# A two-network forward pass on one core: head norms through exp and ln, level sums on VectorE, a skip term on ScalarE, and projections into both kinds of PSUM banks

## The chip, the cores and the metric

The kernel runs on one core of a Trainium2 chip. The metric is device time in microseconds, the median of three runs. A core has five engines that matter here: TensorE (PE in the profile; its weight loads are PEld), VectorE (DVE), ScalarE (ACT), GpSimd (POOL) and SyncE (SP), which only issues DMAs. Each works through its own queue in order, and they meet through semaphores.

## The reference, cut to what matters

The input is 256 tokens of width 1024. Two networks run one after the other, in float32. The first has two layers, each of FFN, mixer, FFN; the mixer of its first layer is a chunked gated linear attention with 4 heads (called the first attention here), that of its second a stick-breaking attention. The second network has one block, in which an S5 state-space branch and an mLSTM branch (4 heads) run from one input projection and are gated and mixed, and then an expert FFN that gathers 16 experts per head for each token. The parts that the change touches:

```
log_a = log_sigmoid(gk_lr @ w_gk2 + b_gk) / 16             # first attention, decay
o = rmsnorm(o, o_norm)                                     # per head, 256 wide
o = o * silu(g);  return o @ w_out
...
h = norm(h) * norm_g + skip * xc                           # mLSTM, per head
y = y * sigmoid(y @ w_glu + b_glu)                         # S5 branch
mixed = sigmoid(g_s) * (y_s @ w_ssm_out) + sigmoid(g_m) * (y_m @ w_ml_out)
```

## The kernel before, in words

Activations lie with the features on the 128 partitions and the 256 tokens along the free axis. All weights come by DMA in pieces of up to 1 MB into two `raw` buffers (`weights`, L145) and are split there into a high and a low part: ScalarE copies the high part `whi` (L198), VectorE subtracts it to get `wlo` (L199). Each of the two has four buffers of 1024 columns. A projection (`acc`, L171) is three matmuls per 128 rows: high by high (L177), high weight by low activation (L178), low weight by high activation (L179). So a piece of weights passes ScalarE, then VectorE, then TensorE.

PSUM is cut into two rings: `bank` (tag `p`, 5 tiles) and `accum` (tag `acc`, 2 tiles). Projections write one or the other; the next user of a tile waits for its evacuation.

The program is written in a natural order, and a scheduler puts each engine's instructions into a fixed queue; `issue_after` holds an instruction behind a named one. What an engine does while it waits is therefore decided before the run.

The first attention (`gla`, L344). The gate's log-sigmoid (`log_sigmoid`, L322) gives P, the sums of the log decays; S starts at zero. Then come 8 levels (l = 0 to 7), each for blocks of B = 2^l tokens: ScalarE takes `eq` and `ek` as exp of half of P and half of S (L417, L418), VectorE and GpSimd scale q and k with them into `qt` (L419) and `kt` (L420), TensorE multiplies them (`put`, L393) and VectorE copies the masked part into s0 and s1 (L394). For the next level, GpSimd adds P's last column of a block to S (L426), and after it VectorE adds it to P (L428). The projections of q, k and v, and of the four gates g, are placed between. After the levels, `weigh` multiplies the scores with v for each of the 4 heads (L441, L442), `rstd256` (L455) squares and sums over the head (L459 to L462), takes the square root on ScalarE (L465) and the reciprocal on VectorE (L469), and `head_norm` (L472) multiplies and splits the result into yh and yl for the output projection. The gates g pass through Silu (L451).

The second block (`block2`, L1112). The S5 scan is 67 steps of five small GpSimd additions and products (L862 to L866), in one chain of its own; its states are copied by ScalarE (`vc`, L875) and multiplied by TensorE into `sy` (L883, L885). Beside it, the mLSTM (`mlstm`, L950) goes through its 4 heads; `third` multiplies the normed head and adds the skip term `sx` (L1096, L1097), then splits it (L1099, L1100). `sx` is computed on VectorE for heads 0 to 2 and on GpSimd for head 3, where also `myl` (L1100) of heads 2 and 3 is made. After the heads come the projections mix and gm (`in_proj`, L908), the S5 output's gate `gl` (one tile for two halves, L1135 reads each half), and ml_out, ssm_out and w_out. After this block the expert part gathers rows `uv` from memory with GpSimd-issued DMAs (L1342).

Of the kernel before, what the change touches and what calls it, by code (L numbers as in the profile page):

```python
# [17 lines left out]
T = 256  # L18
# [14 lines left out]
class Net:  # L33
# [49 lines left out]
    def accum(self, shape, name):  # L83

        return self.ps.tile(shape, F32, tag="acc", name=name, bufs=2)

# [257 lines left out]
    def gla(self, st, x, gnext):  # L344
# [16 lines left out]
        self.log_sigmoid(P, z, self.V("gla_b_gk", 0, 4), [128, 4, T])  # L361
# [47 lines left out]
        for l in range(8):  # L409
# [11 lines left out]
            if l < 7:  # L421
# [4 lines left out]
                nc.gpsimd.tensor_tensor(Sv[:, :, 0, :], Sv[:, :, 0, :],  # L426
# [10 lines left out]
        def weigh(h):  # L437
            ps = self.bank([128, 2, T], name="ov")
            for c in range(2):
                cc = slice(h * 256 + c * 128, h * 256 + (c + 1) * 128)  # L440
                nc.tensor.matmul(ps[:, c, :], v[0][:, cc], s0[:, h, :], start=True, stop=False)  # L441
                nc.tensor.matmul(ps[:, c, 128:256], v[1][:, cc], s1[:, h, :], start=False, stop=True)  # L442
            return ps, self.rstd256(ps)

        weighed = []
        for h in range(4):
            if h % 4 == 0:
                weighed += [weigh(i) for i in range(h, h + 4)]
            for _ in ahead[h]:
                pass  # L450
            nc.scalar.activation(gated[h], gated[h], AF.Silu)  # L451
            self.head_norm(*weighed[h], h, y, gated[h])
        return self.out_proj("gla_w_out", y, x, gnext)

    def rstd256(self, o, e=None):  # L455
# [8 lines left out]
        if e is None:  # L464
            nc.scalar.activation(r, ms, AF.Sqrt, bias=self.eps)  # L465
        else:
            nc.vector.scalar_tensor_tensor(r, ms, 1e-36, e, op0=OP.max, op1=OP.add)
            nc.scalar.activation(r, r, AF.Sqrt)
# [439 lines left out]
    def in_proj(self, st, b0, nb, full, out, fn=None):  # L908
# [4 lines left out]
        for b in range(nb):  # L913
# [6 lines left out]
            else:  # L920
                ps = self.accum([128, 2, T], "ip")
# [28 lines left out]
    def mlstm(self, st, u4):  # L950
# [139 lines left out]
        def third(h, hh, dn):  # L1090
            r = self.rstd256(hh, dn)
            nc.vector.tensor_tensor(hh, hh, r.unsqueeze(1).to_broadcast([128, 2, T]), OP.mult)
            for d in range(2):
                n = 2 * h + d
                sx = self.t2([128, T], "sx")
                (nc.gpsimd if h == 3 else nc.vector).tensor_scalar(sx, xc(n)[:, NM:], self.V("ml_skip", n), None, op0=OP.mult)  # L1096
# [15 lines left out]
    def block2(self, st, x, gnext):  # L1112
# [16 lines left out]
        for b in range(2):  # L1129
            wt = self.weights("ssm_glu", b)  # L1130
            ps = self.bank([128, 2, T], name="gl")
            sg = self.t2([128, 2, T], "sg")
            for j in range(2):
                self.acc(ps[:, j, :], wt, j, lambda k: (yh[:, k, :], yl[:, k, :]))
                nc.scalar.activation(sg[:, j, :], ps[:, j, :], AF.Sigmoid, bias=self.V("ssm_b_glu", 2 * b + j))  # L1135
            nc.vector.tensor_tensor(by4(sg), by4(sg), y[:, 2 * b:2 * b + 2], OP.mult)
            self.split(y2h[:, 2 * b:2 * b + 2, :], y2l[:, 2 * b:2 * b + 2, :], sg)
        for b in range(4):
            wt = self.weights("ml_out", b)
            ps = self.accum([128, 2, T], "mo")  # L1140
# [4 lines left out]
        for b in range(4):  # L1145
            wt = self.weights("ssm_out", b)
            ps = self.accum([128, 2, T], "so")
# [396 lines left out]
```

## Time and profile before

| what | value |
|---|---|
| median of three runs | 1969.02 us (1961.47 to 1969.13) |
| the profiled execution, its own time | 1956.61 us |
| its span | 1954.8 us |
| busy: TensorE, VectorE, ScalarE, GpSimd | 1771.9, 1352.9, 848.2, 657.6 us |
| DMA | 493.53 MB, 252 GB/s in the mean |

The page gives the busy time of each engine and the span in 40 slices. The timelines give each instruction's start and length; the brackets at the end of a line say how long the engine stood idle before it, and what released it. Times in the views count from the start of the span. The first attention lies at about 198 to 312 us, the second block at about 1000 to 1270, the experts from there to the end.

### The profile page before, as it was taken

The page shows a single profiled execution, that of the slowest core. Times are in us where ns is not written, and L with a number is a line of the kernel's source. Part 1 is how long each engine was busy: PE and PEld are TensorE (multiplying, and loading weights), DVE is VectorE, ACT ScalarE, POOL GpSimd, SP SyncE. Part 2 cuts the span into 40 slices and gives each one's busy share as a digit, 9 for nine tenths or more (in the row PEclk, how much of TensorE's full clock was granted, in tenths as well). Part 3 has the DMA queues.
Part 4 walks back from the last instruction along what each step waited for, and adds up shares of the span by engine and source line. Part 5 has one row for each costly group of instructions (what it writes and reads, how often), then busy time and mean ns, then how long its engine had stood idle before and what let it go on. Part 6 is the DMA issues. An engine that isn't in the chain of part 4 may idle for free.

```text
span 1954.8 us, 31080 instructions
## 1 busy us (share of the span) xinstructions
PE 1771.9 (91%) x11905; PEld 1433.5 (73%) x11905; DVE 1352.9 (69%) x2499; ACT 848.2 (43%) x1385; POOL 657.6 (34%) x835
## 2 busy tenths in 40 slices
PE   8999999999999999999999989988777878778776
PEld 7999889999999998899998879963323424334322
DVE  6765678975666567776678465787767676777755
ACT  5444635554544456554444555453222222232223
POOL 4001323041350100200144870245554455555552
PEclk9999999999999999999999999999999999999999
DMA  5555534555654563265465225599999999999996
GB/s 205 191 187 187 182 108 154 198 192 178 213 178 154 191 202 130 89 236 179 167 216 163 71 97 172 184 371 419 420 420 419 419 420 420 420 419 420 420 420 267
DMA packets 81444, 493.53 MB, mean 252 GB/s; under 512 B 14432, under 2 KB 16736, under 8 KB 29072
## 3 DMA queue, kind: packets, MB, share of 16 engines
q0 software_dynamic: 37152, 268.45, 33.2%
q1 hardware_dynamic: 36608, 219.78, 32.7%
q10 hardware_dynamic: 7536, 3.31, 0.8%
q8 instruction: 94, 1.54, 0.3%
q14 instruction: 54, 0.44, 0.1%
HBM read 489.05 MB, written 2.13 MB: 251 GB/s over the span
## 4 chain that ended last, share of the span: by engine, by line
PE 50%; DMA 29%; DVE 8%; POOL 7%; ACT 3%; issue 3%; SPq 0%; ACTq 0%; POOLq 0%; DVEq 0%
DMA uv<-in_peer_uv,route 25%; PE o L177 4%; PE up L177 4%; PE up L179 4%; PE up L178 4%; PE o L179 4%; PE o L178 4%; PE gate L177 4%; PE gate L179 4%; PE gate L178 4%; DVE wlo L199 2%; PE acc L1390 2%; DVE uv L1370 2%; ACT whi L198 1%; POOL V L866 1%
## 5 line engine op out<-in xcount | busy, mean ns | idle before, releaser
L199 DVE TENSOR_TENSOR wlo<-raw,whi 128x1024 fp32r<-128x1024 f32 (+3 forms) x445 | 511.5, 1164 | 188.1 <-ACT whi L198 184.5
L1390 PE MATMUL acc<-uv,dg 128*128 128x512 f32 x1016 | 481.5, 622 | 135.1 <-ACT dg L1388 135.0
L198 ACT ACTIVATE whi<-raw 128x1024 fp32r<-128x1024 f32 (+3 forms) x445 | 424.0, 974 | 359.6 <-PE gate L178 71.9
L1390 PEld LDWEIGHTS acc<-uv,dg 128*128 128x128 f32 x1016 | 190.8, 196 | 420.0 <-ACT dg L1388 222.2
L1342 POOL DMA_INDIRECT uv<-in_peer_uv,route x254 | 325.4, 1281 | 324.7 <-DMA uv<-in_peer_uv,route 196.1
L1370 DVE SCALAR_TENSOR_TENSOR uv<-uv,xn 128x1024 f32<-128x1024 f32 x256 | 313.3, 1224 | 152.7 <-DMA uv<-in_peer_uv,route 149.2
L177 PE MATMUL gate<-xp,whi 128*128 128x256 f32 x704 | 198.4, 282 | 6.8 <-ACT whi L198 6.4
L179 PE MATMUL gate<-xp,wlo 128*128 128x256 f32 x704 | 197.6, 281 | 3.7 <-DVE wlo L199 3.7
L1378 ACT ACTIVATE route<-route 128x2 f32<-128x2 f32 x129 | 26.2, 203 | 400.6 <-DVE uv L1370 400.6
L178 PE MATMUL gate<-xp,whi 128*128 128x256 f32 x704 | 197.2, 280 | 0.5 <-DVE xp L204 0.4
L179 PE MATMUL o<-hh,wlo 128*128 128x256 f32 x704 | 194.8, 277 | 0.0
L179 PE MATMUL up<-xp,wlo 128*128 128x256 f32 x704 | 194.8, 277 | 0.0
L178 PE MATMUL o<-hl,whi 128*128 128x256 f32 x704 | 194.7, 277 | 0.0
L177 PE MATMUL o<-hh,whi 128*128 128x256 f32 x704 | 194.7, 277 | 0.0
L177 PE MATMUL up<-xp,whi 128*128 128x256 f32 x704 | 194.6, 276 | 0.0
L178 PE MATMUL up<-xp,whi 128*128 128x256 f32 x704 | 194.6, 276 | 0.0
L229 POOL TENSOR_TENSOR sumsq<-x 128x256 f32<-128x256 f32 x9 | 6.1, 680 | 412.3 <-DVE x L318 233.8
L177 PEld LDWEIGHTS gate<-xp,whi 128*128 128x128 f32 x704 | 134.5, 191 | 7.9 <-ACT whi L198 6.7
L179 PEld LDWEIGHTS gate<-xp,wlo 128*128 128x128 f32 x704 | 134.3, 191 | 5.0 <-DVE wlo L199 5.0
L178 PEld LDWEIGHTS gate<-xp,whi 128*128 128x128 f32 x704 | 134.5, 191 | 1.2 <-DVE xp L204 1.1
L177 PEld LDWEIGHTS up<-xp,whi 128*128 128x128 f32 x704 | 132.4, 188 | 0.0
L177 PEld LDWEIGHTS o<-hh,whi 128*128 128x128 f32 x704 | 132.3, 188 | 0.0
(459 smaller groups left out, 3782.3 us busy)
## 6 DMA issues: line engine op xcount, KB each, us to landing
raw<-in_ffn_w_up SPq DMA_DIRECT2D x44, 1024.0 KB, 4.8
raw<-in_ffn_w_down SPq DMA_DIRECT2D x64, 704.0 KB, 4.1
raw<-in_ffn_w_gate SPq DMA_DIRECT2D x43, 1024.0 KB, 4.8
raw<-in_w_in SPq DMA_DIRECT2D x18, 1024.0 KB, 4.8
raw<-in_gla_in SPq DMA_DIRECT2D x8, 1024.0 KB, 4.9
raw<-in_sb_in SPq DMA_DIRECT2D x8, 1024.0 KB, 4.8
raw<-in_peer_q SPq DMA_DIRECT2D x8, 1024.0 KB, 8.2
raw<-in_gla_v SPq DMA_DIRECT2D x4, 1024.0 KB, 4.8
```

Of the source, the lines that this page charges most:

```text
L177: nc.tensor.matmul(ps, hi, xh, start=start and n == 0, stop=False)
L178: nc.tensor.matmul(ps, hi, xl, start=False, stop=False)
L179: nc.tensor.matmul(ps, lo, xh, start=False, stop=stop and n == len(steps) - 1)
L198: return (self.nc.scalar.activation(h, src, AF.Copy).ins, self.nc.vector.tensor_tensor(l, src, h.bitcast(F32), OP.subtract).ins)
L199: self.nc.vector.tensor_tensor(l, src, h.bitcast(F32), OP.subtract).ins)
L229: g.tensor_tensor(q, src, src, OP.mult)
L866: g.tensor_tensor(y, y, t[:, 1], OP.add)
L1342: nc.gpsimd.indirect_dma_start(out=out, out_offset=None, in_=table, in_offset=bass.IndirectOffsetOnAxis(ap=ids, axis=0))
L1370: lastdot = nc.vector.scalar_tensor_tensor(u, u, 1.0, xn[i], op0=OP.mult, op1=OP.mult, accum_out=dots[:, k:k + 1]).ins
L1378: gelu = nc.scalar.activation(w[:, ks], dots[:, ks], AF.Gelu_apprx_tanh).ins
L1390: lastv = nc.tensor.matmul(acc[i][b], dg, vt[:, b * 512:(b + 1) * 512], start=False, stop=hd == 7 and k == 14).ins
```

## The change

Six edits, three in the first attention and three in the second block:

- `log_sigmoid` in `gla` is held behind an explicit load of the ScalarE table set number 6, which follows the square root of the norm before.
- The level sums S (L426) move from GpSimd to VectorE.
- The head norms of the first attention take the reciprocal root as exp(-0.5 ln(ms + eps)), both on ScalarE, under the same table set, loaded behind the Silu of gate 1. The Silu of gates 2 and 3 is held behind the last of these exps. `rstd256` stays for the mLSTM alone.
- Head 3's `sx` in the mLSTM moves from GpSimd to ScalarE.
- The projections of `in_proj` (those without the extra tokens), ml_out and ssm_out take `accum` and `bank` in turn (`either`).
- The two halves of `gl` are two tiles.

```diff
+    def either(self, b, shape, name):
+        return self.bank(shape, name=name) if b % 2 else self.accum(shape, name)
...
-        self.log_sigmoid(P, z, self.V("gla_b_gk", 0, 4), [128, 4, T])
+        with self.tc.issue_after(self.load_tables(6, st.sqrt).ins):
+            self.log_sigmoid(P, z, self.V("gla_b_gk", 0, 4), [128, 4, T])
...
-                nc.gpsimd.tensor_tensor(Sv[:, :, 0, :], Sv[:, :, 0, :],
+                nc.vector.tensor_tensor(Sv[:, :, 0, :], Sv[:, :, 0, :],
                                         Pv[:, :, 1, B - 1:B].to_broadcast([128, n, B]), OP.add)
...
-            return ps, self.rstd256(ps)
-
+            return ps
+
+        for h in range(2):
+            for _ in ahead[h]:
+                pass
+            silu = nc.scalar.activation(gated[h], gated[h], AF.Silu).ins
+        tables = self.load_tables(6, silu).ins
         weighed = []
         for h in range(4):
-            if h % 4 == 0:
-                weighed += [weigh(i) for i in range(h, h + 4)]
-            for _ in ahead[h]:
-                pass
-            nc.scalar.activation(gated[h], gated[h], AF.Silu)
+            ps = weigh(h)
+
+            sq = self.t2([128, 2, T], "hsq")
+            nc.scalar.activation(sq, ps, AF.Square)
+            ms = self.bank([128, T], name="hms")
+            nc.vector.tensor_tensor(sq[:, 0, :], sq[:, 0, :], sq[:, 1, :], OP.add)
+            nc.tensor.matmul(ms, self.ones256, sq[:, 0, :], start=True, stop=True)
+            r = self.t2([128, T], "hr")
+            with self.tc.issue_after(tables):
+                nc.scalar.activation(r, ms, AF.Ln, bias=self.eps)
+                lastr = nc.scalar.activation(r, r, AF.Exp, scale=-0.5).ins
+            weighed.append((ps, r))
+        for h in range(4):
+            if h >= 2:
+                for _ in ahead[h]:
+                    pass
+                with self.tc.issue_after(lastr):
+                    nc.scalar.activation(gated[h], gated[h], AF.Silu)
             self.head_norm(*weighed[h], h, y, gated[h])
...
-                ps = self.accum([128, 2, T], "ip")
+                ps = self.either(b, [128, 2, T], "ip")
...
-                (nc.gpsimd if h == 3 else nc.vector).tensor_scalar(sx, xc(n)[:, NM:], self.V("ml_skip", n), None, op0=OP.mult)
+                if h == 3:
+                    nc.scalar.activation(sx, xc(n)[:, NM:], AF.Copy, scale=self.V("ml_skip", n))
+                else:
+                    nc.vector.tensor_scalar(sx, xc(n)[:, NM:], self.V("ml_skip", n), None, op0=OP.mult)
...
-            ps = self.bank([128, 2, T], name="gl")
+            ps = [self.bank([128, T], name="gl") for _ in range(2)]
...
-                self.acc(ps[:, j, :], wt, j, lambda k: (yh[:, k, :], yl[:, k, :]))
-                nc.scalar.activation(sg[:, j, :], ps[:, j, :], AF.Sigmoid, bias=self.V("ssm_b_glu", 2 * b + j))
+                self.acc(ps[j], wt, j, lambda k: (yh[:, k, :], yl[:, k, :]))
+                nc.scalar.activation(sg[:, j, :], ps[j], AF.Sigmoid, bias=self.V("ssm_b_glu", 2 * b + j))
...
-            ps = self.accum([128, 2, T], "mo")
+            ps = self.either(b, [128, 2, T], "mo")
...
-            ps = self.accum([128, 2, T], "so")
+            ps = self.either(b, [128, 2, T], "so")
```

The scheduler sets the queues anew. At three places they differ as follows; the line numbers of the change are higher than those of before (wlo is L203 there, whi L202).

VectorE in the level loop of the first attention, levels 1 to 3, before and then changed:

```order
L419 TENSOR_TENSOR qt_2322<-q,eq 128x256x2
L199 TENSOR_TENSOR wlo<-raw,whi 128x1024
L428 TENSOR_TENSOR P<-P 128x256x2
L199 TENSOR_TENSOR wlo<-raw,whi 128x1024
L428 TENSOR_TENSOR P<-P 128x128x4
L375 TENSOR_TENSOR k<-qk,rstd 128x512
L199 TENSOR_TENSOR wlo<-raw,whi 128x1024
L428 TENSOR_TENSOR P<-P 128x64x8
L199 TENSOR_TENSOR wlo<-raw,whi 128x1024
```

```order
L380 TENSOR_TENSOR k<-qk,rstd 128x512
L203 TENSOR_TENSOR wlo<-raw,whi 128x1024
L431 TENSOR_TENSOR S<-S,P 128x256x2
L433 TENSOR_TENSOR P<-P 128x256x2
L203 TENSOR_TENSOR wlo<-raw,whi 128x1024
L431 TENSOR_TENSOR S<-S,P 128x128x4
L433 TENSOR_TENSOR P<-P 128x128x4
L380 TENSOR_TENSOR k<-qk,rstd 128x512
L203 TENSOR_TENSOR wlo<-raw,whi 128x1024
L431 TENSOR_TENSOR S<-S,P 128x64x8
L433 TENSOR_TENSOR P<-P 128x64x8
L203 TENSOR_TENSOR wlo<-raw,whi 128x1024
```

S now stands on VectorE, right ahead of each P; the splits wlo keep their places between the levels.

ScalarE at the head norms of the first attention (s is s0, hsq the squares, hr the norm, hms its mean square, yh the high part for the output projection), before and then changed:

```order
L451 ACTIVATE g<-g 128x512
L434 ACTIVATE s_2784<-sc 128x4x128
L459 ACTIVATE hsq<-ov 128x512
L465 ACT_TABLE_LOAD
L465 ACTIVATE hr<-hms,eps 128x256
L459 ACTIVATE hsq<-ov 128x512
L198 ACTIVATE whi<-raw 128x1024
L465 ACTIVATE hr<-hms,eps 128x256
L459 ACTIVATE hsq<-ov 128x512
L198 ACTIVATE whi<-raw 128x1024
L465 ACTIVATE hr<-hms,eps 128x256
L459 ACTIVATE hsq<-ov 128x512
```

```order
L453 ACTIVATE g<-g 128x512
L505 ACT_TABLE_LOAD
L439 ACTIVATE s_2785<-sc 128x4x128
L460 ACTIVATE hsq<-ov 128x512
L466 ACTIVATE hr<-hms,eps 128x256
L467 ACTIVATE hr<-hr 128x256
L460 ACTIVATE hsq<-ov 128x512
L202 ACTIVATE whi<-raw 128x1024
L466 ACTIVATE hr<-hms,eps 128x256
L467 ACTIVATE hr<-hr 128x256
L460 ACTIVATE hsq<-ov 128x512
L466 ACTIVATE hr<-hms,eps 128x256
```

The table load has moved ahead of the copy of s0, and each hr has become two rows.

ScalarE around the last mLSTM head and the S5 states (V are the scan's states, its first and second half), before and then changed:

```order
L1099 ACTIVATE myh<-hh 128x512
L468 ACTIVATE hr<-hr 128x256
L198 ACTIVATE whi<-raw 128x1024
L927 ACT_TABLE_LOAD
L927 ACTIVATE mix<-mix 128x512 x2
L1099 ACTIVATE myh<-hh 128x512
L198 ACTIVATE whi<-raw 128x1024 x2
L927 ACTIVATE mix<-mix 128x512
L875 ACTIVATE vc<-V_12149 128x16x31
L875 ACTIVATE vc<-V_12150 128x16x33
```

```order
L202 ACTIVATE whi<-raw 128x1024
L1117 ACTIVATE sx<-xc,vecs 128x256
L1122 ACTIVATE myh<-hh 128x512
L488 ACTIVATE hr<-hr 128x256
L1117 ACTIVATE sx<-xc,vecs 128x256
L202 ACTIVATE whi<-raw 128x1024
L947 ACT_TABLE_LOAD
L947 ACTIVATE mix<-mix 128x512
L202 ACTIVATE whi<-raw 128x1024 x2
L947 ACTIVATE mix<-mix 128x512
L1122 ACTIVATE myh<-hh 128x512
L202 ACTIVATE whi<-raw 128x1024
L895 ACTIVATE vc<-V_12151 128x16x31
```

The two sx are new ahead of the sigmoids of mix. On GpSimd, the two rows of sx that stood between the scan's last addition and myl are gone:

```order
L865 TENSOR_TENSOR V_12150<-V_12150,s5t 128x32
L866 TENSOR_TENSOR V_12150<-V_12150,s5t 128x32
L1096 TENSOR_SCALAR sx<-xc,vecs 128x256 x2
L1100 TENSOR_TENSOR myl<-hh,myh 128x512 x2
L229 TENSOR_TENSOR sumsq<-x_84 128x256
```

```order
L885 TENSOR_TENSOR V_12152<-V_12152,s5t 128x32
L886 TENSOR_TENSOR V_12152<-V_12152,s5t 128x32
L1123 TENSOR_TENSOR myl<-hh,myh 128x512 x2
L233 TENSOR_TENSOR sumsq<-x_84 128x256
L236 TENSOR_TENSOR sq<-x_84 128x256
```

What stays there is myl, behind the scan as before.

## Rows read from the trace of the kernel before

**Rows 1.** page, busy time of the span, then granted TensorE clock and DMA share by slice
```profile
PE 1771.9 (91%) x11905; PEld 1433.5 (73%) x11905; DVE 1352.9 (69%) x2499; ACT 848.2 (43%) x1385; POOL 657.6 (34%) x835
...
PEclk9999999999999999999999999999999999999999
DMA  5555534555654563265465225599999999999996
```

**Rows 2.** chain that ended last in order of time: start us, us, engine, work
```profile
1340.00 18.27 DMA uv<-in_peer_uv,route
```

**Rows 3.** timeline of PE: start, us, engine, line, op, out<-in, count [idle before <-releaser]
```profile
236.85 0.50 PE L192 MATMUL v<-wlo,xp 128*128 128x512 f32 x1 [1.29 <-DVE wlo L199]
...
256.12 2.97 PE L393 MATMUL sc<-qt,kt 128*128 128x128 f32 x16 [2.15 <-DVE v L195]
...
1151.60 0.36 PE L177 MATMUL ip<-xp,whi 128*128 128x256 f32 x1 [1.61 <-DVE mix L925]
...
1166.25 0.58 PE L179 MATMUL ip<-xp,wlo 128*128 128x256 f32 x1 [5.66 <-DVE wlo L199]
...
1173.64 0.27 PE L885 MATMUL sy<-vc,ca 64*64 64x64 f32 x1 [1.59 <-ACT vc L875]
...
1207.13 0.39 PE L177 MATMUL gl<-yh,whi 128*128 128x256 f32 x1 [2.12 <-ACT sg L1135]
...
1242.22 0.36 PE L177 MATMUL so<-yh,whi 128*128 128x256 f32 x1 [1.66 <-DVE mt L1151]
```

**Rows 4.** busy time by stretch: from:to, us, each engine's busy us (instructions), PEclk, DMA share, GB/s
```profile
223.45:234.40 10.95, 10.95 (x50) 8.83 (x48) 6.46 (x7) 5.12 (x7) 5.99 (x5) 1.00 0.47 154
234.40:250.23 15.83, 12.90 (x53) 9.41 (x53) 11.05 (x13) 9.35 (x13) 5.15 (x6) 1.00 0.37 126
258.00:260.00 2.00, 2.00 (x12) 2.00 (x11) 2.00 (x4) 0.00 (x0) 0.83 (x1) 0.50 0.63 160
300.00:312.00 12.00, 9.59 (x71) 8.61 (x72) 9.93 (x18) 5.78 (x9) 0.00 (x0) 1.00 0.20 68
1166.20:1171.20 5.00, 4.95 (x22) 4.77 (x22) 3.44 (x3) 3.57 (x5) 1.13 (x1) 0.50 0.64 215
```

**Rows 5.** timeline of VectorE (DVE)
```profile
234.97 0.69 DVE L428 TENSOR_TENSOR P<-P 128x512 f32<-128x512 f32 x1 [3.60 <-POOL S L426]
...
286.63 1.75 DVE L469 RECIPROCAL hr<-hr 128x256 f32<-128x256 f32 x1 [2.64 <-ACT hr L465]
...
1130.31 1.24 DVE L199 TENSOR_TENSOR wlo<-raw,whi 128x1024 fp32r<-128x1024 f32 x1 [0.31 <-ACT whi L198]
...
1162.68 0.70 DVE L1097 SCALAR_TENSOR_TENSOR hh<-hh,vecs,sx 128x256 f32<-128x256 f32 x1 [10.03 <-POOL sx L1096]
```

**Rows 6.** timeline of GpSimd (POOL)
```profile
230.32 3.52 POOL L420 TENSOR_TENSOR kt<-k,ek 128x512 f32<-128x512 f32 x2 [1.41 <-DVE k L375]
...
240.03 1.08 POOL L426 TENSOR_TENSOR S<-S,P 128x512 f32<-128x512 f32 x1 [1.99 <-ACT ek L418]
...
1130.54 1.12 POOL L866 TENSOR_TENSOR V<-V,s5t 128x32 f32<-128x32 f32 x1
...
1160.24 0.26 POOL L866 TENSOR_TENSOR V<-V,s5t 128x32 f32<-128x32 f32 x1
...
1161.71 1.84 POOL L1096 TENSOR_SCALAR sx<-xc,vecs 128x256 f32<-128x256 f32 x2
```

**Rows 7.** timeline of ScalarE (ACT)
```profile
212.95 1.28 ACT L330 ACT_TABLE_LOAD   x1
...
241.87 0.63 ACT L417 ACTIVATE eq<-P 128x512 f32<-128x512 f32 x1 [0.96 <-DVE P L428]
...
286.12 0.47 ACT L465 ACTIVATE hr<-hms,eps 128x256 f32<-128x256 f32 x1
...
1169.59 4.00 ACT L875 ACTIVATE vc<-V 128x496 f32<-128x496 f32 x4
...
1256.29 0.51 ACT L203 ACTIVATE xp<-x,vecs 128x256 fp32r<-128x256 f32 x1 [0.56 <-DVE x L318]
```

More of the change, by code (lines that the diff above doesn't have):

```diff
@@ L442, in weigh, with rstd256 @@
                 nc.tensor.matmul(ps[:, c, 128:256], v[1][:, cc], s1[:, h, :], start=False, stop=True)
-            return ps, self.rstd256(ps)
+            return ps
[4 more added lines that the diff above has]
+        tables = self.load_tables(6, silu).ins
         weighed = []
         for h in range(4):
-            if h % 4 == 0:
-                weighed += [weigh(i) for i in range(h, h + 4)]
-            for _ in ahead[h]:
-                pass
-            nc.scalar.activation(gated[h], gated[h], AF.Silu)
+            ps = weigh(h)
[15 more added lines that the diff above has]
+                    nc.scalar.activation(gated[h], gated[h], AF.Silu)
             self.head_norm(*weighed[h], h, y, gated[h])
         return self.out_proj("gla_w_out", y, x, gnext)
-    def rstd256(self, o, e=None):
+    def rstd256(self, o, e):
         nc = self.nc
@@ L463, in rstd256 @@
         r = self.t2([128, T], "hr")
[L464 to L468, printed above, removed]
+        nc.vector.scalar_tensor_tensor(r, ms, 1e-36, e, op0=OP.max, op1=OP.add)
+        nc.scalar.activation(r, r, AF.Sqrt)
         nc.vector.reciprocal(r, r)
```

## The prediction

> **What bounds the kernel now.** I read the page first: TensorE is busy for 91% of the span and its clock is full almost throughout, while the DMA engines are full only from the 27th slice on [rows 1]. The chain of waits, read next, shows the same split: up to the gathers it runs mostly through TensorE and what TensorE waits for, and then through the gathers of expert rows, in steps such as 18.27 us [rows 2]. The change touches only the first part. The gathers start when the routes exist, so what TensorE's path loses or saves before them moves the whole second part. The price of each edit is therefore the TensorE time that it frees, and I list TensorE's own waits [rows 3] and the stretches in which it falls behind its rate [rows 4]. At full clock the 48 matmuls of 512 columns of one half of v take 10.95 us [rows 4], 0.228 each; one of 256 columns I count as half of that, 0.114.
>
> The profiled execution took 1956.6 us (span 1954.8). The median of the three runs shown is 1969.0, 12.4 above it, with runs from 1961.5 to 1969.1. I work out a difference on the profiled one and take it from the median.
>
> **The level sums (L426).** In each level GpSimd adds to S once ScalarE's ek has read it, and VectorE's addition to P waits for GpSimd. The weights of v are split on VectorE between these additions, so v's matmuls run at the loop's pace: the first half of v took 10.95 us, the second 15.83 [rows 4], with TensorE waiting for wlo [rows 3]. GpSimd idles 1.99 before an S and takes 1.08 for it, a period of 3.07; once S stood behind two kt products of 3.52 together, and VectorE waited 3.60 for it [rows 5, 6]. The change removes seven GpSimd additions and adds seven on VectorE. Their nearest row is P's addition, same shape and stride, 0.69 [rows 5]; GpSimd's 1.08 is the upper bound, and below 0.69 I see no reason. A level is then eq 0.63 [rows 7], ek as much, overlapping to about 1.2, then S and P 1.4: 2.6 us. A split feeds 12 matmuls, 12 x 0.228 = 2.74. So the loop becomes slightly faster than TensorE, and the second half of v should take 10.95 plus 0.6 for the small transposes of rstd instead of 15.83: **4.3 us** less, ends 2 (a level stays at 3.07 and only the long wait goes) and 4.3.
>
> After v, TensorE waited 2.15 us for v's evacuation, which stood behind a split whose weights had not landed, and then ran at half clock (granted 0.50) [rows 3, 4]: 16 score products took 2.97 us, which at 0.114 are 1.8, and the next projections lose about 0.4, together 1.5. With the splits earlier, the evacuation follows v at once; that is up to 3.7. But from there VectorE has the masked copies, the scalings and the splits of the score stage to do, and no longer a stalled TensorE to catch up with. I take 2 off: **1.7**, ends 0 and 3.7.
>
> **Log-sigmoid.** Two of three table loads of 1.28 us go from ScalarE [rows 7], and exp and ln run back to back. No TensorE wait names them, so alone this is worth nothing; its cover is the projections of q and k. It lets the level loop begin some 2.6 us earlier, which helps the 4.3.
>
> **The head norms.** Four reciprocals of 1.75 us leave VectorE [rows 5]; four exps come to ScalarE, each about the square root's 0.47 [rows 7], and ln takes the square root's place at the same price; ends for each 0.4 and 0.7 (the double shape's 0.63). The table load moves ahead of the copy of s0, while TensorE still multiplies scores and gates. What is late next: the exp of the last head stands behind a split that waits for a weight buffer, then come a Silu table load, the third and fourth gates, and the last yh. From 300 to 312 us TensorE issued 71 matmuls in 12.00 us [rows 4]; they are 8.1 of work, so 3.9 are lost. The last two gates' own chain (scaling, Silu, product, norm, split) still ends behind TensorE, since the second Silu load is still there. I take half: **2.0**, ends 0 and 3.9.
>
> **The last head's skip term.** GpSimd's two sx, 1.84 us together, stand behind the S5 scan; VectorE waited 10.03 us for them [rows 5, 6], TensorE 5.66 for the split behind that, then ran at half clock, and its S5 output (sy) began in earnest only at 1173.64 [rows 3]. On ScalarE an sx costs about the 0.51 of a scaled copy of the same shape [rows 7] (GpSimd's 0.92 at most). Then TensorE's projections finish: the 22 to 23 that were left at 1160.5 take 2.6 us at full clock, less the 1.61 that TensorE waited for a bank before them [rows 3]: 1161.5. What is late next is the scan. Its last step that is read ends at 1160.5. Beside a split of 1.24 us a scan operation took 1.12 instead of 0.26 [rows 5, 6]; three splits now run beside its end: 3 x 0.87 = 2.6, so 1163.1. Of the four copies vc (4.00 [rows 7]) the first can go early; three and a sigmoid of 0.6 remain: sy starts at 1166.7, 6.9 earlier. TensorE idles 5 us before it; after a like pause the clock was at half, and those 23 matmuls took 5.0 us [rows 4] instead of 2.6, so I charge sy 2.4. **4.5**, ends 0 and 9.
>
> The Trainium skill, SBUF — State Buffer, section "Who interferes with whom", speaks against this part: a VectorE instruction with two SBUF inputs locks out a GpSimd instruction that reads SBUF until it has finished. By it every split and every two-input step of the last head would hold the scan for its full length, an estimated 5 us instead of 2.6, and the sum below would be 12.7 instead of 15.1. The trace agrees that the scan is held, but shows 0.87 of a split of 1.24.
>
> **Both kinds of banks.** The wait of gl for sg (2.12 [rows 3]) is one for ScalarE's read of the other half of the same tile; separate tiles take it away: 2.1. The wait of 1.66 before the last blocks of ssm_out [rows 3] is for an accumulator that VectorE's mt empties; the mt itself is no earlier than VectorE's queue lets it be, and the next projection needs its product, so I count 0.5 of it. **2.6**, ends 0 and 3.8. The bank ring of five gets more users; its cover is that the head norms and the gate products have released theirs by then. The order of the DMA queue is the same.
>
> Sum: 4.3 + 1.7 + 2.0 + 4.5 + 2.6 = **15.1 us, say 15**: 1969.0 - 15 = **1954.0**.
>
> **Rivals.** (1) VectorE becomes the bound. It takes 7 x 0.69 = 4.8 us more in the first attention and at the scan's end holds GpSimd. Then v gives 2, the score stage and the norms nothing, the scan 1.7 and the banks 2.1: 5.8, so 1963.2. For it: VectorE's waits for ScalarE and TensorE stay. Against it: 7 us of reciprocals and the long waits leave its queue. (2) A new ring of waits in the level loop, slower than before. If the split ahead of ek on ScalarE waits for a weight buffer that TensorE frees only after the wlo queued behind S on VectorE, a level takes 12 matmuls 2.74, whi 1.0, eq and ek 1.2, S and P 1.4, wlo 1.2: 7.5 instead of 3.07. Over the five levels beside v that is +22, while the other parts give 10.8: 1980. It decides from a level of 5.2 us on. Against it: there are four buffers of either half, and ScalarE's eq waited only for P [rows 7]. (3) The change doesn't do what it says: the freed time is waited away at the next weight or at the gathers, 1969. Against it: the DMA engines are half idle in that part [rows 1].
>
> **Chances.** Forecast 0.60, rival 1 0.25, rival 2 0.05, rival 3 0.10. About 0.5% (10 us) is what a measurement of this kernel can tell from no change. Nearly all of the forecast's own range, 1946 to 1960, is faster than that, and rival 1 is now and then. Hence faster 0.62, same 0.32, slower 0.06. The upper ends add up to 4.3 + 3.7 + 3.9 + 9 + 3.8 = 24.7, the lower to 2; within that, and with the spread of the runs, I give 1943 to 1966, which leaves out rival 2, most of rival 3 and a rest.
>
> **What would show it.** A level period near 2.6 us and no TensorE wait for wlo in v; no half clock at 258; no 10-us wait of VectorE, and sy 4 to 7 us earlier, counted from the projections before it; wider scan steps at its end; no wait of gl for sg. I am wrong if TensorE has new waits for VectorE in the score stage, if sy starts less than 3 us earlier, or if the first gathers do not start 10 us earlier.

## The result, and the profile after

| | before | changed |
|---|---|---|
| median of 20 runs (us) | 1967.07 | 1951.27 |
| lowest to highest (us) | 1959.71 to 1978.77 | 1946.59 to 1965.62 |
| profiled execution's own time, span (us) | 1956.61, 1954.8 | 1948.90, 1947.1 |

The ratio is 0.9938, with a 95% interval of 0.992 to 0.9955: 8.9 to 15.7 us less, 12.2 in the middle. The medians lie 15.8 apart, the two profiled spans only 7.7. The forecast was 1954.0, 15 us less, with a range of 1943 to 1966: the time lies 2.7 us below the forecast. Of these, 1.9 come from the base: the kernel before now measures 1967.1, where the forecast had started from 1969.0. The rest of this text asks whether the steps were right too, and why the two traces differ by half of what the medians do. Two executions of the experiments, one of the twelve of e3 and one of the six of e8, took 6.2 ms for a reason that is not known; the ratios leave them out.

The page of the changed kernel, to be laid beside [rows 1]: TensorE's work is the same, 12 us left GpSimd.

```profile
PE 1771.1 (91%) x11905; PEld 1435.5 (74%) x11905; DVE 1353.0 (69%) x2502; ACT 848.0 (44%) x1389; POOL 645.3 (33%) x826
...
PEclk9999999999999999999999999999999999999998
DMA  6555525555555553264465235599999999999996
```

TensorE's timeline of the changed kernel (columns as in [rows 3]). Of the waits shown there, those for wlo in v, for a bank at the mix projections, for the split behind the skip term, for sg and for mt are gone. The wait behind v became one of 1.50 for VectorE's qt; S5's output now waits for ScalarE's vc, that is for the scan; and out of block 2 comes a new wait for the split mxl.

```profile
254.67 2.02 PE L398 MATMUL sc<-qt,kt 128*128 128x128 f32 x16 [1.50 <-DVE qt L424]
...
307.71 0.39 PE L183 MATMUL o<-yh,wlo 128*128 128x256 f32 x1 [0.39 <-DVE wlo L203]
...
1163.70 0.47 PE L905 MATMUL sy<-vc,ca 64*64 64x64 f32 x2 [3.71 <-ACT vc L895]
...
1166.17 0.37 PE L905 MATMUL sy<-vc,ca 64*64 64x64 f32 x1 [1.99 <-ACT vc L895]
...
1237.02 0.40 PE L182 MATMUL o<-mxl,whi 128*128 128x256 f32 x1 [1.29 <-DVE mxl L203]
```

Busy time by stretch (columns as in [rows 4]): all of v in two pieces, the score products that ran at half clock before, the end of the head norms, S5's output, and the matmuls behind the wait for mxl. In the first four TensorE is busy almost throughout, and the 0.50 at 258 us has become 1.00. Two stretches at half clock (granted 0.50) are left in the second block: one still lies at the end of the scan, now on S5's output, and the one behind mxl is new.

```profile
221.81:233.00 11.19, 11.19 (x51) 8.94 (x50) 10.91 (x11) 7.04 (x12) 5.25 (x4) 1.00 0.48 180
233.00:244.70 11.70, 11.70 (x54) 9.69 (x55) 8.76 (x12) 6.43 (x10) 0.00 (x0) 1.00 0.64 199
254.60:257.60 3.00, 2.93 (x26) 2.96 (x27) 2.29 (x4) 0.00 (x0) 0.73 (x1) 1.00 0.12 44
290.00:301.70 11.70, 11.70 (x100) 11.53 (x99) 9.38 (x14) 6.27 (x9) 0.00 (x0) 1.00 0.52 179
1162.20:1168.90 6.70, 3.21 (x53) 3.02 (x54) 1.81 (x2) 6.33 (x8) 3.78 (x8) 0.50 0.01 2
1237.50:1240.50 3.00, 3.00 (x16) 3.00 (x16) 3.00 (x5) 0.63 (x1) 0.00 (x0) 0.50 0.39 109
```

VectorE's timeline of the changed kernel: a level from one P to the next takes 233.82 - 231.18 = 2.64 us where it was 3.07; then, in the score stage, a split slowed to 2.09, five masked copies and the scaling qt for which TensorE waits.

```profile
231.18 0.69 DVE L433 TENSOR_TENSOR P<-P 128x512 f32<-128x512 f32 x1
...
233.09 0.69 DVE L431 TENSOR_TENSOR S<-S,P 128x512 f32<-128x512 f32 x1
233.82 0.69 DVE L433 TENSOR_TENSOR P<-P 128x512 f32<-128x512 f32 x1
...
248.72 2.09 DVE L203 TENSOR_TENSOR wlo<-raw,whi 128x1024 fp32r<-128x1024 f32 x1
250.73 3.23 DVE L399 COPY_PREDICATED s<-masks,sc 128x512 f32<-128x512 uint32 x5
253.85 1.28 DVE L424 TENSOR_TENSOR qt<-q,eq 128x512 f32<-128x512 f32 x2
```

ScalarE's: logarithm and exponential of a head norm, the Silu table load that stayed between the norms and the last two gates, and one sx of the last head.

```profile
286.95 0.47 ACT L466 ACTIVATE hr<-hms,eps 128x256 f32<-128x256 f32 x1 [1.31 <-PE hms L463]
...
288.28 0.41 ACT L467 ACTIVATE hr<-hr 128x256 f32<-128x256 f32 x1
...
290.92 1.28 ACT L474 ACT_TABLE_LOAD   x1
...
1143.21 0.49 ACT L1117 ACTIVATE sx<-xc,vecs 128x256 f32<-128x256 f32 x1
```

GpSimd's, at the end of the scan: an operation beside a split, and what now follows the scan.

```profile
1153.67 1.20 POOL L884 TENSOR_TENSOR s5t<-V,s5a 128x16 f32<-128x16 f32 x1
...
1163.50 0.25 POOL L886 TENSOR_TENSOR V<-V,s5t 128x32 f32<-128x32 f32 x1
1163.71 2.50 POOL L1123 TENSOR_TENSOR myl<-hh,myh 128x512 fp32r<-128x512 f32 x2
```

**A measure by stage.** Whole executions scatter by some 19 us, and the parts are worth 1 to 7, so I compare stages of the profiles, between events that every kernel has: rs is the square root on ScalarE in a layer's norm, hr on ScalarE the root in a head's norm, psc the first score product of the routing. Start: when rs of the first attention's norm begins. First attention: from there to rs of the norm behind it. Feed-forward 2: from rs of its norm to the first hr of the second block. Block 2: from that hr to the last Gelu (S5's output), and, in the last column, from the same hr to the first psc. All in us, each difference of two start times.

| profile of | start | first attention | feed-forward 2 | hr to last Gelu | hr to first psc |
|---|---|---|---|---|---|
| before | 200.60 | 139.68 | 276.09 | 59.71 | 155.83 |
| changed | 198.97 | 132.20 | 285.01 | 54.73 | 149.07 |
| e1 levels | 199.69 | 134.54 | 278.96 | 61.21 | 156.56 |
| e2 norms | 199.12 | 137.75 | 282.84 | 62.20 | 158.58 |
| e3 skip | 207.25 | 139.95 | 279.56 | 54.37 | 149.91 |
| e4 banks | 201.54 | 139.67 | 280.09 | 58.30 | 152.86 |
| e5 changed again | 207.06 | 131.61 | 277.99 | 56.00 | 149.10 |
| e6 maps in four | 200.78 | 132.84 | 281.03 | 56.12 | 151.29 |
| e7 gate block ahead | 200.90 | 132.77 | 281.38 | 58.37 | 146.41 |
| e8 both | 208.09 | 131.44 | 275.39 | 58.31 | 145.21 |
| e9 log-sigmoid | 207.03 | 138.81 | 276.52 | 61.53 | 157.27 |
| e10 skip and banks | 200.71 | 139.78 | 279.36 | 56.05 | 151.91 |
| e11 three edits | 200.78 | 132.76 | 276.86 | 58.31 | 145.68 |
| e12 skip on VectorE | 208.10 | 132.84 | 279.31 | 56.18 | 150.37 |

The first attention takes 139.67 to 139.95 in the four profiles that leave it alone and 131.44 to 132.84 in the seven that have the whole change there: 139.8 - 132.4 = 7.4 us less. Block 2 takes 157.1 in the mean of the four without its edits (before, e1, e2, e9) and 149.8 in the mean of the three that have exactly the change's (changed, e5, e6): 7.2 less. From the first psc to the end all fourteen lie between 679.1 and 679.9, and between the first attention and feed-forward 2 between 502.2 and 504.6. Together the two stages give **14.6 us**, within the 8.9 to 15.7 of the whole runs. What the first profile of the changed kernel lacks to that, it lost in feed-forward 2, which the change does not touch. That the change gives nothing back there is not shown: the four profiles with the change and this stage as before (changed, e5, e7, e12) take 278.0 to 285.0, the seven without the whole change (before, e1 to e4, e9, e10) 276.1 to 282.8.

### The profile page after: what moved, and what is told of

It reads as the page before. It is cut to its first block, busy times and chain, and to the rows that moved or that the text cites. A ratio compares the mean times of both kernels' runs of the same rounds, so it can differ in the third digit from the quotient of the medians.

```text
span 1947.1 us, 31062 instructions
## 1 busy us (share of the span) xinstructions
PE 1771.1 (91%) x11905; PEld 1435.5 (74%) x11905; DVE 1353.0 (69%) x2502; ACT 848.0 (44%) x1389; POOL 645.3 (33%) x826
## 4 chain that ended last, share of the span: by engine, by line
PE 52%; DMA 29%; DVE 6%; POOL 6%; issue 3%; ACT 3%; SPq 0%; POOLq 0%; ACTq 0%; DVEq 0%
DMA uv<-in_peer_uv,route 25%; PE up L182 4%; PE up L181 4%; PE up L183 4%; PE gate L181 4%; PE gate L183 4%; PE gate L182 4%; PE o L181 4%; PE o L182 4%; PE o L183 4%; PE acc L1413 3%; DVE wlo L203 2%; POOL V L886 1%; ACT whi L202 1%; DMA raw<-in_ffn_w_down 1%
## 5 line engine op out<-in xcount | busy, mean ns | idle before, releaser
L203 DVE TENSOR_TENSOR wlo<-raw,whi 128x1024 fp32r<-128x1024 f32 (+3 forms) x445 | 513.4, 1170 | 191.1 <-ACT whi L202 189.8
L202 ACT ACTIVATE whi<-raw 128x1024 fp32r<-128x1024 f32 (+3 forms) x445 | 424.0, 974 | 359.6 <-PE gate L182 74.5
L183 PEld LDWEIGHTS gate<-xp,wlo 128*128 128x128 f32 x704 | 134.5, 191 | 4.4 <-DVE wlo L203 4.4
L183 PEld LDWEIGHTS o<-hh,wlo 128*128 128x128 f32 x704 | 132.2, 188 | 1.6 <-DVE wlo L203 1.6
```

Of the source, the lines that this page charges most:

```text
L183: nc.tensor.matmul(ps, lo, xh, start=False, stop=stop and n == len(steps) - 1)
L202: return (self.nc.scalar.activation(h, src, AF.Copy).ins, self.nc.vector.tensor_tensor(l, src, h.bitcast(F32), OP.subtract).ins)
L203: self.nc.vector.tensor_tensor(l, src, h.bitcast(F32), OP.subtract).ins)
```

## The experiments

**e1 to e4: one part each.**

e1, the level sums:

```diff
-                nc.gpsimd.tensor_tensor(Sv[:, :, 0, :], Sv[:, :, 0, :],
+                nc.vector.tensor_tensor(Sv[:, :, 0, :], Sv[:, :, 0, :],
```

> The kernel before with one edit: S of the level loop on VectorE. Theory A (GpSimd's addition sets the loop's period): the period of a level falls from 3.07 us to about 2.6, the second half of v takes 11 to 12 us instead of 15.8, the 2.15 us wait behind v and the half clock after it go; 4.3 + 1.7 = 6.0 us in the stage, of which 1 us may be missing because the loop still begins behind the third table load. Theory B (VectorE becomes the bound): v gives 2 us, the score stage nothing. In one profiled execution the stage's own length decides, from rs of the norm ahead of it to the last score product; between whole executions a difference that neither theory has can lie in how fast TensorE runs the feed-forward layers.

Measured: 1959.32 us, ratio 0.9978 (0.9961 to 0.9996); the first attention 139.8 - 134.5 = 5.2 us shorter. v takes 22.9 us, as in the changed kernel, and the wait behind v is 0.96 instead of 2.15, with no half clock behind it:

```profile
250.50 2.02 PE L393 MATMUL sc<-qt,kt 128*128 128x128 f32 x16 [0.96 <-DVE v L195]
...
255.99 2.02 PE L393 MATMUL sc<-qt,kt 128*128 128x128 f32 x16 [0.64 <-DVE qt L419]
```

Theory A holds: GpSimd's addition set the period. By theory B only 2 us would have gone. The second row is the grain of truth in B: VectorE is late with qt.

e2, the head norms (the block from the first gates to the last, as in the change, without its other edits):

```diff
-            return ps, self.rstd256(ps)
+            return ps
...
+            with self.tc.issue_after(tables):
+                nc.scalar.activation(r, ms, AF.Ln, bias=self.eps)
+                lastr = nc.scalar.activation(r, r, AF.Exp, scale=-0.5).ins
...
```

> The kernel before with one edit: the four head norms as exp(-0.5 ln) and the gates' Silu around them. Theory A: the reciprocals were on the way of the gates, 2.0 us from the first head norm to the last yh. Theory B: the second Silu load and the last two gates' chain end as late as before: 0. That the norms are worth their full 4 x 1.75 = 7 us would be seen as 5 us or more.

Measured: 1963.42 us, ratio 1.001 (0.9993 to 1.0026); the first attention 2.0 us shorter, as in theory A. The whole runs do not show it: their interval allows 1.4 us less at most. In the profile the 2.0 is overtaken by the untouched feed-forward 2, 6.8 us longer than before. So the stage confirms the term; that it reaches the end by itself is not shown.

e3, the skip term:

```diff
-                (nc.gpsimd if h == 3 else nc.vector).tensor_scalar(sx, xc(n)[:, NM:], ...
+                if h == 3:
+                    nc.scalar.activation(sx, xc(n)[:, NM:], AF.Copy, scale=self.V("ml_skip", n))
+                else:
+                    nc.vector.tensor_scalar(sx, xc(n)[:, NM:], ...
```

> The kernel before with one edit: the last head's two sx on ScalarE. Theory A: VectorE's wait of 10.03 us and TensorE's of 5.66 us go, the scan ends some 2.6 us later because splits run beside it, S5's output comes 4 to 7 us earlier than the projections before it tell, 4.5 us in all. Theory B (VectorE holds GpSimd's scan): the scan ends 5 us or more later, 1.7 us in all.

Measured: 1961.51 us, ratio 0.9986 (0.9967 to 1.0006); block 2 takes 149.9 instead of 157.1, the largest single part, and in this one profile already all that the changed kernel gains in this block (149.8). The scan ends 45.1 us after the first hr instead of 41.9 (41.9 to 42.2 in before, e1, e2, e4 and e9; 45.1 to 45.2 in the changed kernel, e5, e6 and e10): 3.2 us later, nearer to theory A's 2.6 than to B's 5. S5's output starts 45.0 us after the hr, where the changed kernel has 45.1, but behind shorter waits (3.71 and 1.99 there):

```profile
1176.36 0.33 PE L885 MATMUL sy<-vc,ca 64*64 64x64 f32 x2 [1.62 <-ACT vc L875]
...
1178.30 0.27 PE L885 MATMUL sy<-vc,ca 64*64 64x64 f32 x1 [1.61 <-ACT vc L875]
```

The 1.66 that the mix projections still wait for a bank in e3 does not delay it, since the scan is what is late. The half clock behind these waits lasts 3.4 us in e3 (granted 0.50 from 1178.5 to 1181.9) and 6.8 in the changed kernel.

e4, the banks (and either as in the change):

```diff
-                ps = self.accum([128, 2, T], "ip")
+                ps = self.either(b, [128, 2, T], "ip")
...
-            ps = self.bank([128, 2, T], name="gl")
+            ps = [self.bank([128, T], name="gl") for _ in range(2)]
```

> The kernel before with the bank edits alone (ip, mo and so take both kinds by turns, gl has a tile for each j). Theory A: the 2.12 us wait of gl for sg goes, and 0.5 us of the 1.66 us wait of the last blocks: 2.6 us. Theory B: only the wait of gl goes, 2.1 us, and the first free bank does nothing because the mix projections wait for the weight split anyway. Rival: the transposes and gate products that share the ring of five wait instead, 0 or slower.

Measured: 1962.41 us, ratio 0.9997 (0.9981 to 1.0014); block 2 takes 152.9, 3.0 us less than before and 4.2 less than the mean. Theory A, a little more than expected. The wait of the mix projections for a bank (1.61, [rows 3]) went too, but the time came back as a longer wait behind the skip term, so this part of it was worth nothing while the skip term was late:

```profile
1170.56 0.58 PE L183 MATMUL ip<-xp,wlo 128*128 128x256 f32 x1 [8.05 <-DVE wlo L203]
```

In whole runs the four parts are worth less than their stages say: 4.3, -2.0, 2.7 and 0.6 us by their ratios, together 5.7, where the whole change gives 12.2. The gains that the stages show for e2, e3 and e4 against the mean (2.0, 7.2 and 4.2) lie above what the intervals allow (1.4, 6.5 and 3.7). Each part was profiled once, and the cause of the difference stays open. So the stages show where each part acts, and the whole runs show a gain for the sum and for e1 alone.

**e5 to e8: where the first profile lost its gain, and two edits against it.** e5 is the changed kernel, unaltered.

> The changed kernel once more, as the base of the other three runs of this set. Theory A (the change gives some 15 us, and what one execution has more or less lies in TensorE's pace and half clocks elsewhere): its whole-run ratio is that of the first measurement, 0.992 to 0.9955; in its profile the first attention and the second block are again 7 to 8 us and 6 to 8 us shorter than before, whatever the whole span says. Theory B (the change itself gives back some 8 us between 320 and 1120 us, as its first profile seemed to say): the same loss stands at the same places again.

Measured: 1951.68 us, ratio 0.9937 (0.9916 to 0.9957). The first attention and block 2 are again 131.6 and 149.1; feed-forward 2 is 278.0 and not 285.0. Theory A: the loss was that execution's, not the change's. Three things made it up, worked out from the start times of the same instructions in both traces. First, a run of 48 matmuls of 36 columns (gw, the gate maps), and the projections behind it, at half clock: 3.1 us. The stretch in the kernel before, in the changed kernel and in e5:

```profile
896.00:901.50 5.50, 5.50 (x52) 5.50 (x51) 1.84 (x3) 1.69 (x2) 0.00 (x0) 1.00 0.24 98
```

```profile
889.00:895.80 6.80, 6.80 (x34) 6.80 (x34) 2.19 (x3) 0.00 (x0) 0.00 (x0) 0.51 0.00 0
```

```profile
895.30:901.00 5.70, 5.70 (x54) 5.70 (x53) 1.98 (x4) 1.69 (x2) 0.00 (x0) 1.00 0.22 92
```

Second, TensorE at full granted clock but some 4% slower for 100 us: 4.8 us, with two short waits (0.53 and 0.68) in it. The same 70 us of projections without a wait, in the kernel before and in the changed kernel, 621 matmuls against 597:

```profile
910.00:980.00 70.00, 70.00 (x621) 70.00 (x620) 46.41 (x58) 32.98 (x44) 8.49 (x11) 1.00 0.53 178
```

```profile
910.00:980.00 70.00, 70.00 (x597) 70.00 (x596) 45.75 (x57) 31.76 (x43) 10.47 (x13) 1.00 0.50 168
```

Third, 0.94 and 0.82 us of waiting for GpSimd at the norm of block 2, where the kernel before waited 0.41: 1.0 of it came through. Together 8.9, which is 285.01 - 276.09.

e6, the gate maps:

```diff
-        for h in range(2):
-            ps = self.bank([128, 4, 2, 36], name="gw")
-            for m in range(4):
+        for h in range(4):
+            ps = self.bank([128, 2, 2, 36], name="gw")
+            for m in range(2):
...
+            yield
```

> The changed kernel with the 48 narrow gate-map matmuls (36 columns) in four groups of 12, one behind each of four feed-forward blocks, in place of one run of 48. Theory A: the half clock that stands on this run in the profiles of the change and of three of its four parts comes from the run itself; in four groups it does not appear, and the median falls by 2 to 4 us against the changed kernel. Theory B: the clock falls by chance, whatever TensorE does then: no difference, and half clocks at the groups or elsewhere.

Measured: 1945.11 us, ratio 0.9901 (0.9883 to 0.9919), 6.6 below e5 in the median. In the 10 us from the start of the unbroken run the granted clock was below full in eight of eleven profiles (0.65 to 0.74 in the changed kernel, e1, e2, e4, e10 and e12, 0.83 in e3 and e9; 1.00 in the kernel before, e5 and e7), and it was full around all four groups in e6, e8 and e11. That speaks for theory A, though three profiles are few and an unbroken run kept full clock in three as well. The profile of e6 itself is no shorter in feed-forward 2 (281.0, e5 278.0): it waited longer at block 2's norm (1.85 and 0.82 us, e5 0.93 and 1.02) and then ran at half clock from 1017.9 to 1021.3. How much of the 6.6 comes from the maps is not shown.

e7, a gate projection ahead of S5's output:

```diff
+        self.in_proj(st, 14, 1, False, gm, AF.Sigmoid)
         y = self.s5_output(u4, V).rearrange("p q j n -> p q n j")
-        self.in_proj(st, 14, 4, False, gm, AF.Sigmoid)
+        self.in_proj(st, 15, 3, False, lambda k, n: gm(k + 2, n), AF.Sigmoid)
```

> The changed kernel with the first of the four gate projections (gm, 48 matmuls of 256 columns, 5.4 us) ahead of S5's output. Theory A: TensorE waits for the scan's end there (3.71 and 1.99 us, then half clock), so the block fills the wait: sy starts no later, its half clock goes, the projections behind it end 5 to 6 us earlier, and the routes with them, unless S5's trip through DRAM is then what the glu projections wait for: minus 3 to minus 6 us. Theory B: the block's two weight splits on VectorE hold the scan, sy starts 2 us later and the glu projections wait for it: minus 2 to plus 1.

Measured: 1945.93 us, ratio 0.991 (0.9893 to 0.9928). The median is 5.8 below e5's, at the far end of theory A's window. In the stages both theories are half right. Block 2 takes 146.4, 2.7 less than in the changed kernel, and S5's output runs at full clock; but the scan ends 49.3 us after the first hr instead of 45.2, held by the block's splits, and the last Gelu comes 2.3 to 3.6 us later. What more the whole runs gain is not accounted for. GpSimd's last scan operations in e7:

```profile
1162.49 1.26 POOL L883 TENSOR_TENSOR s5t<-V,s5a 128x16 f32<-128x16 f32 x1
...
1165.44 1.19 POOL L886 TENSOR_TENSOR V<-V,s5t 128x32 f32<-128x32 f32 x1
```

e8 has both edits.

> Both edits of the two runs before on the changed kernel. If they are independent their gains add up: minus 5 to minus 9 us against the changed kernel, a ratio to the kernel before of about 0.989.

Measured: 1945.2 us, ratio 0.9895 (0.9871 to 0.992), 6.5 below e5. That is the ratio that was expected, but the gains do not add up: each edit alone had given about as much (6.6 and 5.8). In whole runs both are no different from either, though the profiled stages are among the shortest of the table.

**e9 to e12.** e9, the table load ahead of log-sigmoid alone:

```diff
-        self.log_sigmoid(P, z, self.V("gla_b_gk", 0, 4), [128, 4, T])
+        with self.tc.issue_after(self.load_tables(6, st.sqrt).ins):
+            self.log_sigmoid(P, z, self.V("gla_b_gk", 0, 4), [128, 4, T])
```

> The kernel before with one edit: one table load (exp and ln) ahead of log-sigmoid. What decides is the profiled length of the first attention, from the rs of its norm to the rs of the norm behind it: 139.7 us before and in the two runs that leave it alone, 134.5 with the level sums alone, 137.8 with the head norms alone, 131.4 to 132.8 in four profiles of the whole change. Theory A (it is worth nothing alone, but lets the level loop begin earlier): 139 to 139.7 here. Theory B (the loop's start is on the path in the kernel before too): 137 or less.

Measured in one run: 1964.69 us; the first attention takes 138.8, 1.0 less. A little under theory A's window and well above B's: nearly nothing alone. With e1's 5.2 and e2's 2.0 that is 8.2, the whole gave 7.4.

e10, the edits of e3 and e4 together on the kernel before.

> The kernel before with the skip term on ScalarE and the bank edits, the first attention as before. From the first hr of the second block to the first psc, four profiles without these edits show 155.8, 156.6, 158.6 and, with the banks alone, 152.9; the skip term alone gives 149.9, the whole change 149.1. Theory A (the two edits share a wait: the bank of the mix projections is waited for only where VectorE is late for the skip term): 149 to 150, not the 146 or so of a sum of both; the piece up to the last Gelu is 54 to 56, the rest 93 to 95. Theory B (they add up): 146 to 147.

Measured in one run: 1957.65 us; 56.05 to the last Gelu and 151.9 to the first psc. They do not add up (theory B is out): with the banks it is no shorter than e3's 149.9 with the skip term alone, and it came 2 us above theory A's window. Of these it shows 2.16 on a wait that is 0.41 in the changed kernel:

```profile
1244.60 0.38 PE L181 MATMUL o<-mxh,whi 128*128 128x256 f32 x1 [2.16 <-ACT mxh L202]
...
1246.27 0.58 PE L182 MATMUL o<-mxl,whi 128*128 128x256 f32 x1 [1.29 <-DVE mxl L203]
```

e11, e8 with a third edit:

```diff
...
-        self.sum_squares(n, src, st.squares[1])
+        if n < 7:
+            self.sum_squares(n, src, st.squares[1])
+        else:
+            st.last = self.t2([128, T], "sq7")
+            nc.scalar.activation(st.last, src, AF.Square)
...
+            nc.tensor.matmul(ps[:, NM:], self.ones, st.last, start=False, stop=True)
...
```

> The changed kernel with the gate maps in four, the gate block ahead of S5's output, and a third edit: the last square of the second block's norm on ScalarE, added by a matmul of its own, and the memset of tiny ahead of the stage. In four of five profiles of the changed kernel and its variants TensorE waits 0.9 to 1.85 and 0.8 to 1.0 us for GpSimd there, where GpSimd's square takes 1.3 to 1.5 us beside a split, 0.61 without, and half clock follows in one of them. Theory A: these waits and their half clock go, feed-forward 2 takes 275 to 277 us, 2 to 3 us less in the median than with two edits: a ratio of 0.987 to 0.989 to the kernel before. Theory B (the reciprocal and the weights that follow are late anyway): no difference to the two edits, 0.9895.

Measured: 1942.45 us, the lowest median of the study, ratio 0.9897 (0.9877 to 0.9917), no different from e8's. The waits do go. In e6:

```profile
1015.80 0.70 PE L647 MATMUL mm<-sumsq,tiny 128*128 128x256 f32 x2 [1.85 <-POOL tiny L644]
1017.32 0.70 PE L648 MATMUL mm<-sumsq,ones 128*128 128x256 f32 x2 [0.82 <-POOL sumsq L237]
```

and in e11:

```profile
1015.30 0.70 PE L653 MATMUL mm<-sq,ones 128*128 128x256 f32 x2 [0.41 <-ACT sq L642]
```

Feed-forward 2 takes 276.9, as theory A said; that it is worth 2 us in the median is not shown.

e12, the changed kernel with the last head's sx on VectorE:

```diff
-                    nc.scalar.activation(sx, xc(n)[:, NM:], AF.Copy, scale=self.V("ml_skip", n))
+                    nc.vector.tensor_scalar(sx, xc(n)[:, NM:], self.V("ml_skip", n), None, op0=OP.mult)
```

> The changed kernel with the last head's two sx on VectorE, as for the other heads, in place of ScalarE. Theory A (what counts is that they leave GpSimd's queue behind the scan): the piece to the last Gelu stays within 1 us of the changed kernel's 54.7 to 56.1. Theory B (VectorE is the tight engine there): the 0.6 us of the two sx and the splits pushed back by them show as 1 to 2 us more.

Measured in one run: 1954.01 us; 56.2 to the last Gelu. Theory A: the gain is that the skip term left the queue behind the scan; which of the other two engines takes it matters little.

## Why the prediction was right

| step | forecast | measured in the stages | by |
|---|---|---|---|
| v | 4.3 | 3.9 (26.78 to 22.89 us) | changed kernel |
| behind v | 1.7 | 1.9 (end of v to the first sum of squares) | changed kernel |
| levels (v and behind v) | 6.0 | 5.8; 5.2 alone | changed kernel; e1 |
| log-sigmoid | 0 | 1.0 alone | e9 |
| head norms | 2.0 | 2.0 alone; 2.8, less 1.2 given back | e2, changed kernel |
| skip term | 4.5 | 5.5 to the last Gelu; 7.2 alone | changed, e5, e6; e3 |
| banks | 2.6 | 1.7 from the last Gelu on; 3.0 to 4.2 alone; nothing beside the skip term | changed, e5, e6; e4; e3 and e10 |
| sum | 15.1 | 14.6 | |

The sum is nearer than its terms. The skip term gave 1.0 more than forecast and the banks 0.9 less, and that these cancel is luck.

- **The level sums** went as worked out: S on VectorE costs P's 0.69, a level 2.64, v runs at TensorE's rate. That v lacks 0.4 of the forecast is no wait: TensorE is busy through all of it, and e1's v takes the same 22.9, so the forecast's 10.95 and 11.55 for the halves were that much too short. One level is slow, an S of 1.81 and a P of 1.69 at 225.70 and 227.55, beside GpSimd's two kt of 3.89 together; TensorE did not wait for it.
- **Behind v** I took 2 us off for VectorE's copies and scalings. The row at 254.67 shows that work: TensorE still waits, 1.50 instead of 2.15, now for qt; the half clock behind it is gone. This was one of the signs by which I would have been wrong ("new waits for VectorE in the score stage"). It stands there, but its cost was in the term.
- **The head norms** end with the second Silu load at 290.92 and the last yh, as said. Not foreseen: 1.2 us of it goes again from the last yh to the next norm, 0.7 of it in the output projection, where TensorE waits for wlo at 307.71 (0.39) and at 311.02 (0.31).
- **The skip term**: the scan was named as what is late next, and is: 3.2 us later instead of 2.6. S5's output starts 6.8 us earlier after the first hr (45.1 instead of 51.9), as forecast (6.9). The piece to the last Gelu is 55.6 in the mean of the changed kernel, e5 and e6, against 61.2 in before, e1, e2 and e9, 5.5 us less; the forecast's 4.5 had charged S5's output 2.4 for half clock, and of that not all came. By the rule of the Trainium skill, SBUF — State Buffer, section "Who interferes with whom", the hold would have been an estimated 5 us. The trace agrees that splits hold GpSimd (20 scan operations over 0.9 us instead of 17), but the 3.2 us are 1.1 for each of the three new ones, nearer to the 0.87 per split that the row gave.
- **The banks**: the wait of gl for sg is gone with its 2.12, and mt's 1.66; but 1.29 and 0.41 come back as waits for mxl and mxh, and behind them TensorE runs 3.4 us at half clock (the row at 1237.50). The bank of the mix projections gave nothing of its own once the skip term was out of the way: it only makes TensorE's wait for the scan longer (3.71 and 1.99 instead of e3's 1.62 and 1.61), and the half clock on S5's output with it. So the 1.7 from the last Gelu on is about what the piece ahead of it loses against e3 (54.4 there, 55.6 in the mean of the three): over the block the banks add nothing to the skip term that these profiles show (149.8 and 149.9). This is the term that the forecast had wrong: it counted the waits that go, and not those that come in their place.

Rival 1 is out for the stages it named: VectorE has the level sums, v gives 3.9 and not 2, the skip term 5.5 and not 1.7. Rival 2's level of 5.2 us or more does not occur. Rival 3 is what the first pair of traces would have suggested, and e5 shows it wrong. The third sign, the first gathers 10 us earlier, failed as it was put (the first gather of uv 7.9 us earlier in the first pair, 5.3 in e5): a time counted from the start of the execution carries 7 to 9 us of chance from stages that the change does not touch. It should have been put as stage lengths.

## What to carry to other kernels

Count a gain in the stage in which it arises, between two events that both kernels have, and only then in the whole time: here the two stages of the change repeat to between 0.3 and 3 us, those that it does not touch to 9, whole executions to 19. Two waits in a row on the same engine, as a bank and a late split, are worth one of them. A step that stood behind a long serial chain on GpSimd, without needing its result, gained as much on ScalarE as on VectorE; and VectorE's splits beside the chain lengthened it.

## What the runs showed of the hardware that I had not expected

- **TensorE has two paces at full granted clock.** A 256-column matmul takes 0.113 us in most stretches (100 us over the 885 below) and 0.118 (over the 851) in some of 100 to 200 us, with a granted clock of 1.00 (the higher of its two levels, 2.4 GHz) and nothing waited for; the kernel and the place do not decide it. The start column of the table shows it: 199.0 to 201.5 in nine profiles, 207.0 to 208.1 in five, e5 and the changed kernel being the same program. The same 100 us, without a wait, in the changed kernel and in e5:

```profile
50.00:150.00 100.00, 100.00 (x885) 100.00 (x884) 65.89 (x75) 47.08 (x55) 0.62 (x1) 1.00 0.56 188
```

```profile
50.00:150.00 100.00, 100.00 (x851) 100.00 (x850) 64.40 (x72) 46.45 (x54) 0.62 (x1) 1.00 0.52 179
```

What sets it was not found. With 7 to 8 us for the first 200 us, it is large enough for a good part of the scatter of whole runs; that it is the cause there is not shown, since few of them were profiled.

- **The clock fell to half (1.2 GHz) in a run of narrow matmuls in which TensorE did not wait:** 48 matmuls of 36 columns, 5.4 us, in eight of eleven profiles; the same 48 in groups of 12, in none of three. What sets it was not found.
- **An earlier split can cost time.** Where block 2's first weights are split early, VectorE's split runs beside GpSimd's last steps of the norm. The addition behind the last square then takes 1.55 to 1.76 us instead of 0.73 (changed, e2, e3, e5, e6, e7), the square itself in three of these 1.52 instead of 0.61 (e2, e6, e7), and TensorE waits for them. In e6, GpSimd's row behind the 1.85 us shown above, and the split beside it:

```profile
1014.08 1.52 POOL L236 TENSOR_TENSOR sq<-x 128x256 f32<-128x256 f32 x1 [0.23 <-DVE x L635]
```

```profile
1013.92 2.76 DVE L203 TENSOR_TENSOR wlo<-raw,whi 128x1024 fp32r<-128x1024 f32 x2
```
